# First block of a hybrid decoder: low parts of the weights made by accumulating transfers, head gains applied to the transposed outputs

## The chip, the core and the metric

The kernel runs on one core of a Trainium2 chip. A core has a matmul engine (TensorE, PE in the profile; its weight loads are PEld), a vector engine (VectorE, DVE), a scalar engine (ScalarE, ACT), a general engine (GpSimd, POOL) and a sync engine (SyncE, SP). Each takes its instructions in the order of its own queue. Transfers between DRAM and the core's memory are issued from one of these queues and run beside the engines. The metric is the device time of one execution in microseconds (us); lower is better. The kernel before was run three times.

## What is computed

A decoder trunk of one layer, 2048 tokens, width 1024. The layer has a token mixer (three groups of heads: retention, HGRN2 and GLA, all fed by one input projection and closed by one output projection) and a gated channel mixer with a short convolution. Only the token mixer matters here:

```python
def token_mixer(h, w_in, w_gla_up, b_gla, lb, head_gain, w_out, pos):
    proj = h @ w_in
    (rq, rk, rv, rg, hq, hf, hi, hg, aq, ak, av, ag, alow) = jnp.split(proj, offs, axis=-1)
    ...
    o = jnp.concatenate([o_r, o_h.astype(o_r.dtype), o_a.astype(o_r.dtype)], axis=-1) * head_gain
    return o @ w_out

    # in the layer
    h = rms_norm(x) * (1.0 + sc1) + sh1
    x = x + g1 * token_mixer(h, ...)
```

`head_gain` is a vector over the 1024 columns of `o`, that is, over the rows of `w_out`.

## The kernel before

**Arithmetic.** PE multiplies in a rounded 32-bit format. To keep the precision of 32-bit floats, each operand is split in a high part (the value rounded to that format) and a low part (value minus high part), and each product takes three matmuls: high by high, high by low, low by high (`split3`, lines 244 to 248). So each weight needs a high part, made by ACT as a cast, and a low part, made by DVE as a subtraction.

**Blocks.** The sequence is cut in four blocks of 512 tokens. In each block the mixer's work comes as units, in the order of `ORDER` (line 35): HGRN2 pair 0, GLA, HGRN2 pairs 1 to 3, retention pairs 0 and 1. A unit multiplies its pieces of the input projection by the normalised input `h` (`cf_gemm`, `tf_gemm` and `tf512`), and then runs a chain of smaller matmuls and DVE and ACT steps (`gated` or `retention`) that ends in an output `o`, transposed by PE into `oT` (`transposed`, line 555). The output projection follows in two halves (`out_half`, line 902): the first at the end of the block, the second after the first unit of the next block.

**Pieces.** A piece of weights is 128 x 1024 floats, 512 KB. `piece` (line 212) and, for units that use 512 columns at once, `tf512` (line 286) load it from DRAM into one of two raw buffers (`wraw`), cast it into one of three `whi` tiles and subtract into one of three `wlo` tiles. A `whi` or `wlo` tile comes free when the matmuls of the piece three before are over. The first time that a piece is used, in block 0, its low part is also written to a DRAM scratch by `keep` (line 205, issued on SP); later blocks load the low part from there (`key + "l" in kept`) and no longer subtract. The eight pieces of the output projection are scaled by `head_gain`: ACT makes the high part in four steps of 256 columns with the gain as a scale (L236), DVE the low part in four (L239), both parts are kept, and later blocks load both.

**Other users of the raw buffers.** The adaLN weights (`wada`) pass through the same two raw buffers. `ada` (line 193) has DVE multiply and reduce one of them, and `piece` and `tf512` do one such load and reduction ahead of their own work while the list `later` has entries: eight in block 0 after the first unit, and more in blocks 1 and 2.

**Start.** `startup` (line 376) does the first unit's projections by hand. Eight slices k of `x` are normalised one after another (`scaled`, `high` and `low`: DVE, ACT, DVE), each followed by DVE reductions of adaLN weights (`cond`), and the matmuls of each slice are issued as soon as it and its weights are there. The weights are `f`, `q` (whole), `v0` (slices 0 to 3) and `v1` (slices 4 to 7). `cast` makes a high part, `low_part` a low part. `plan` (line 456) says after which slice each is made: `f` after slice 0, `q` after 1, `v0` after 2, `v1` after 4.

**Order of the instructions.** PE's order is that of the program, everywhere. In the start, that of DVE, ACT and SP is too. Everywhere else a scheduler orders each engine's queue when the program is built, from priorities (`high_priority(offset)` moves the work under it ahead) and from its own idea of durations. POOL has the memsets of attention tiles (`at`, line 606, and `new_qbd`, line 505) in its queue, and issues no transfers.

The a4k tiles hold `oT`, the attention tiles and, in the start, the parts of `v1`; eight of them exist.

Of the kernel before, what the change touches and what calls it, by code (L numbers as in the profile page):

```python
# [9 lines left out]
F32 = mybir.dt.float32  # L10
F32R = mybir.dt.float32r
I32 = mybir.dt.int32
U32 = mybir.dt.uint32
AF = mybir.ActivationFunctionType
ALU = mybir.AluOpType
# [7 lines left out]
NB = SEQ // TB  # L23
# [15 lines left out]
V_BADA, V_BGLA, V_LB, V_HG, V_CW, V_CB, V_FG, NV = 0, 48, 49, 53, 61, 193, 237, 245  # L39
# [15 lines left out]
class Clock:  # L55
# [15 lines left out]
    def adv(self, us):  # L71
        self.t += us
        while self.due and self.due[0][0] <= self.t:
            self._next()
# [26 lines left out]
def trunk(ctx, tc, xT, vecs, cvec, cst, rope, msk, wada, win, walow, wgla, wout, wup, wdown, out):  # L101
    nc = tc.nc
# [15 lines left out]
    def acc_ps(name):  # L118
        return pp.tile([P, 512], F32, tag="acc", name=name, bufs=4)
# [6 lines left out]
    def late_ps(name):  # L126
        return pp.tile([P, 512], F32, tag="late", name=name, bufs=2)
# [10 lines left out]
    V, S, G, T = nc.vector, nc.scalar, nc.gpsimd, nc.tensor  # L138

    vec = pc.tile([P, NV], F32, tag="vec", name="vec")  # L140
# [52 lines left out]
    def ada(m, raw=None):  # L193

        if raw is None:
            raw = ada_load(m, False)
        V.tensor_tensor_reduce(raw[:], raw[:], c_act[:], 1.0, bada1[:, m:m + 1], op0=ALU.mult, op1=ALU.add,
                               accum_out=mod[:, m:m + 1])
# [4 lines left out]
    kept = {}  # L203

    def keep(key, t):

        kept[key] = pdr.tile([P, 1024], F32, tag=f"kept{key}", name=f"kept{key}")
        nc.sync.dma_start(kept[key][:], t.bitcast(F32))

    later = []  # L210

    def piece(src, name, key, gain=None, ahead=50):

        if later:
            ada(later.pop(0))
        with tc.high_priority(offset=ahead):
            hi = pw.tile([P, 1024], F32R, tag="whi", name="h" + name)
            lo = pw.tile([P, 1024], F32R, tag="wlo", name="l" + name)
            if key + "h" in kept:
                nc.sync.dma_start(hi[:].bitcast(F32), kept[key + "h"][:])  # L220
                nc.sync.dma_start(lo[:].bitcast(F32), kept[key + "l"][:])
                return hi, lo
            raw = pw.tile([P, 1024], F32, tag="wraw", name="r" + name, bufs=NRAW)
            nc.sync.dma_start(raw[:], src)
            if gain is None:
                S.copy(hi[:], raw[:])
                if key + "l" in kept:
                    nc.sync.dma_start(lo[:].bitcast(F32), kept[key + "l"][:])
                else:
                    V.tensor_tensor(lo[:], raw[:], hi[:], op=ALU.subtract)  # L230
                    keep(key + "l", lo[:])
            else:
                n = 1024 // len(gain)
                for i, g in enumerate(gain):
                    sl = slice(i * n, (i + 1) * n)
                    S.activation(hi[:, sl], raw[:, sl], AF.Copy, scale=g)  # L236
                for i, g in enumerate(gain):
                    sl = slice(i * n, (i + 1) * n)
                    V.scalar_tensor_tensor(lo[:, sl], raw[:, sl], g, hi[:, sl], op0=ALU.mult, op1=ALU.subtract)  # L239
                keep(key + "h", hi[:])  # L240
                keep(key + "l", lo[:])
        return hi, lo

    def split3(ps, lhs, rhs, first, last, more=False):

        T.matmul(ps, lhs[0], rhs[0], start=first, stop=False, skip_group_check=more)  # L246
        T.matmul(ps, lhs[0], rhs[1], start=False, stop=False, skip_group_check=more)  # L247
        T.matmul(ps, lhs[1], rhs[0], start=False, stop=last, skip_group_check=more)  # L248

    h = [None] * KD  # L250
# [35 lines left out]
    def tf512(name, i):  # L286

        pss = [acc_ps(f"ps{name}_{c}") for c in range(NCH)]
        for q4 in range(4):
            half, sub = q4 // 2, q4 % 2  # L290
            src = win[i + half:i + half + 3:2][:, :, sub * 512:(sub + 1) * 512].rearrange("a p n -> p a n")
            if later:
                ada(later.pop(0))
            with tc.high_priority(offset=50):
                raw = pw.tile([P, 2, 512], F32, tag="wraw", name=f"r{name}_{q4}", bufs=NRAW)
                nc.sync.dma_start(raw[:], src)
                hi = pw.tile([P, 2, 512], F32R, tag="whi", name=f"h{name}_{q4}")
                lo = pw.tile([P, 2, 512], F32R, tag="wlo", name=f"l{name}_{q4}")
                S.copy(hi[:], raw[:])
                key = f"t{i}_{q4}l"  # L300
                flat = lo[:].rearrange("p a n -> p (a n)")
                if key in kept:
                    nc.sync.dma_start(flat.bitcast(F32), kept[key][:])
                else:
                    V.tensor_tensor(lo[:], raw[:], hi[:], op=ALU.subtract)
                    keep(key, flat)
            for c in range(NCH):
                cs = slice(c * P, (c + 1) * P)
                for kk in range(2):
                    k = half * 4 + sub * 2 + kk  # L310
                    sl = slice(kk * 256, (kk + 1) * 256)
                    split3(pss[c][:].rearrange("p (a n) -> p a n", a=2), (h[k][:, 0, cs], h[k][:, 1, cs]),
                           (hi[:, :, sl], lo[:, :, sl]), k == 0, k == KD - 1)
                    adv(3 * M512)
        return pss
# [24 lines left out]
    def sumsq(acc, x, k, name, sl=slice(0, TB), first=None):  # L340
        if k == 0 if first is None else first:
            S.activation(acc[:, sl], x[:, sl], AF.Square)
        else:
            sq = late(f"sq{name}{k}")
            S.activation(sq[:, sl], x[:, sl], AF.Square)
            V.tensor_tensor(acc[:, sl], acc[:, sl], sq[:, sl], op=ALU.add)
# [18 lines left out]
    def x_tile(name, k):  # L365

        if k % 2 == 0:
            pair[0] = px.tile([P, SB], F32, tag="xy", name=name, bufs=4)
        return pair[0][:, (k % 2) * TB:(k % 2 + 1) * TB]
# [6 lines left out]
    def startup():  # L376


        x, W, pending = [], {}, []
# [12 lines left out]
            W[name] = [*t, raw, i]  # L392

        def cast(name):
            S.copy(W[name][0][:], W[name][2][:])

        def low_part(name):
            hi, lo, raw, i = W[name]
            V.tensor_tensor(lo[:], raw[:], hi[:], op=ALU.subtract)

        def cond(m):
            ada(m, raws.pop(m))
# [13 lines left out]
        ps = late_ps("ssn1_0")  # L416
# [7 lines left out]
        ps = late_ps("bcn1_0")  # L424
# [35 lines left out]
        for k, (ld, first, then, wl) in enumerate(plan):  # L460
# [9 lines left out]
            if k in (1, 4):  # L470
                name = "v0" if k == 1 else "v1"
# [83 lines left out]
    def transposed(b, pos, o, name):  # L555

        ps = late_ps("oT" + name)
        for c in range(NCH):
            T.transpose(ps[:, c * P:(c + 1) * P], o[:, c, :], ident)
        oT = pa.tile([P, 2, TB], F32R, tag="a4k", name="oT" + name)  # L560
        S.copy(oT[:, 0, :], ps[:])
        V.tensor_tensor(oT[:, 1, :], ps[:], oT[:, 0, :], op=ALU.subtract)
        oTs[b][pos] = oT

    def attn_out(name, b, attn, v, q, Sst, qn=None):
# [334 lines left out]
        nc.sync.dma_start(d[:, 2:4, :].rearrange("p a n -> p (a n)"), t1[:])  # L900

    def out_half(b, half, acc=None, after_pieces=None):
        hg = [vec[:, V_HG + 4 * half + k:V_HG + 4 * half + k + 1] for k in range(4)]
        ops = [oTs[b][4 * half + k] for k in range(4)]
        for i in range(4):
            wp = piece(wout[half * 4 + i], f"wo{b}_{half}_{i}", f"o{half * 4 + i}", gain=hg, ahead=250 if (b, half) == (0, 0) else 600 if (b, half) == (NB - 1, 1) else 50)
            if i == 3 and after_pieces:
                after_pieces()
            for m in (2 * i, 2 * i + 1):
                if half == 0:  # L910
                    x1[m] = x_tile(f"x1_{b}_{m}", m)
                    nc.sync.dma_start(x1[m], xT[b, :, m, :])
                ps = acc_ps(f"y{b}_{half}_{m}")
                for k in range(4):
                    ws = slice(k * 256 + (m % 2) * P, k * 256 + (m % 2) * P + P)
                    split3(ps[:], (wp[0][:, ws], wp[1][:, ws]), (ops[k][:, 0, :], ops[k][:, 1, :]), k == 0, k == 3)
                    adv(3 * M512)
                with tc.high_priority(offset=HOT):
                    V.scalar_tensor_tensor(x1[m], ps[:], G1[:, m:m + 1], x1[m], op0=ALU.mult, op1=ALU.add)
                if half == 1:  # L920
                    with tc.high_priority(offset=HOT):
                        sumsq(acc, x1[m], m, f"n2_{b}_")
# [116 lines left out]
    for b in range(NB):  # L1039
        pos = 0  # L1040
# [308 lines left out]
    ahead = up_inputs(B)  # L1349
# [109 lines left out]
```

## Time and profile before

| | |
|---|---|
| time, three runs | 2579.37 us median (2577.66 to 2580.24) |
| the profiled execution | 2574.37 us, span of its instructions 2572.6 us |
| PE busy | 2497.9 us, 97% |
| DVE busy | 1986.9 us, 77% |
| ACT busy | 1116.9 us, 43% |
| POOL busy | 144.1 us, 6% |
| memory moved | 533.88 MB, mean 208 GB/s |

A row of a group says: line, engine, operation, output and inputs by the program's names, shapes, count; then the busy time and the mean of one in ns; then how long the engine stood idle ahead of these and what ended the waits. A row of waits says who waited for whom: us in total, times, the longest. A row of a timeline begins with start and duration in us. A row of stages begins with the stretch and its length, and gives busy us and instruction counts of PE, PEld, DVE, ACT and POOL, the granted clock of PE, the mean busy share of the transfer engines and the rate. A row of transfers gives count, size and the median us from issue to landing. The ends of matmuls are modelled.

### The profile page before, as it was taken

What the parts mean: (1) busy time and instruction counts of PE and PEld (TensorE: products, weight loads), DVE (VectorE), ACT (ScalarE), POOL (GpSimd) and SP (SyncE); (2) the same over time, 40 slices, a digit from 0 to 9 for tenths busy, and PEclk for the clock granted to TensorE, in tenths of its full rate; (3) what the DMA queues carried; (4) which work ended last, traced back from release to release, by engine and by line L of the source; (5) the groups of instructions that cost most, each with busy time, mean ns of one, the idle gap of its engine ahead of it and who ended that gap; (6) DMA issues with size and microseconds to landing.
All of it is one profiled execution on the core that took longest, in us unless ns stands there. A gap on an engine that the chain in (4) does not pass through costs nothing.

```text
span 2572.6 us, 37082 instructions
## 1 busy us (share of the span) xinstructions
PE 2497.9 (97%) x13132; PEld 2130.8 (83%) x13132; DVE 1986.9 (77%) x3627; ACT 1116.9 (43%) x1897; POOL 144.1 (6%) x246
## 2 busy tenths in 40 slices
PE   5999999999999999999999999999999999999997
PEld 4798878998889888998778888888878888888886
DVE  8778986868778786887778888887678778778565
ACT  3333434433343234433355554555444554555442
POOL 1000010000000000000010000000000001010000
PEclk9999999999999999999999999999999999999998
DMA  8543656765687856877665445477675544447653
GB/s 304 198 155 132 215 216 231 273 219 178 215 306 269 295 174 213 312 265 258 213 232 175 157 138 167 149 268 247 206 234 166 157 143 148 153 132 266 210 194 115
DMA packets 231753, 533.88 MB, mean 208 GB/s; under 512 B 25072, under 2 KB 26128, under 8 KB 231568
## 3 DMA queue, kind: packets, MB, share of 16 engines
q1 hardware_dynamic: 231568, 531.52, 60.7%
q8 instruction: 103, 1.69, 0.3%
q14 instruction: 82, 0.67, 0.1%
HBM read 397.72 MB, written 133.69 MB: 207 GB/s over the span
## 4 chain that ended last, share of the span: by engine, by line
PE 88%; DVE 7%; DMA 3%; issue 1%; ACT 1%; SPq 0%; DVEq 0%; ACTq 0%
PE X L246 6%; PE X L247 6%; PE X L248 6%; PE lvh L622 4%; PE Z L247 3%; PE Z L246 3%; PE Z L248 3%; PE dX L248 3%; PE dX L246 3%; PE dX L247 3%; PE psqkvgr L248 2%; PE psqkvgr L246 2%; PE psqkvgr L247 2%; PE dY L246 2%; PE dY L248 2%; PE dY L247 2%
## 5 line engine op out<-in xcount | busy, mean ns | idle before, releaser
L246 PE MATMUL X<-B,A 128*128 128x512 f32 x572 | 223.4, 391 | 1.4 <-ACT u L1242 1.4
L247 PE MATMUL X<-B,A 128*128 128x512 f32 x572 | 222.9, 390 | 0.3 <-DMA B<-made 0.3
L248 PE MATMUL X<-B,A 128*128 128x512 f32 x572 | 222.6, 389 | 0.0
L973 DVE TENSOR_TENSOR dA<-rd,dA 128x512 fp32r<-128x512 f32 x154 | 106.1, 689 | 96.3 <-ACT dA L972 96.0
L972 ACT CAST dA<-rd 128x512 fp32r<-128x512 f32 x154 | 95.7, 621 | 154.6 <-PE dY L248 52.6
L973 DVE TENSOR_TENSOR A<-s,A 128x512 fp32r<-128x512 f32 x176 | 120.5, 686 | 40.2 <-ACT A L972 39.9
L246 PE MATMUL psvgh<-hvgh,ha 128*128 128x256 f32 x480 | 139.9, 291 | 0.0
L246 PE MATMUL dX<-dB,dA 128*128 128x512 f32 x352 | 136.9, 389 | 0.0
L247 PE MATMUL dX<-dB,dA 128*128 128x512 f32 x352 | 136.9, 389 | 0.0
L248 PE MATMUL dX<-dB,dA 128*128 128x512 f32 x352 | 136.9, 389 | 0.0
L248 PE MATMUL psvgh<-hvgh,ha 128*128 128x256 f32 x480 | 135.6, 283 | 0.0
L972 ACT CAST A<-s 128x512 fp32r<-128x512 f32 x176 | 108.6, 617 | 62.3 <-PE Z L248 46.8
L247 PE MATMUL psvgh<-lvgh,ha 128*128 128x256 f32 x480 | 135.6, 283 | 0.0
L246 PEld LDWEIGHTS X<-B,A 128*128 128x128 f32 x572 | 107.4, 188 | 24.9 <-ACT u L1242 2.2
L247 PEld LDWEIGHTS X<-B,A 128*128 128x128 f32 x572 | 107.4, 188 | 23.3 <-DMA B<-made 1.4
L248 PEld LDWEIGHTS X<-B,A 128*128 128x128 f32 x572 | 107.4, 188 | 22.4
L246 PE MATMUL Z<-B,A 128*128 128x512 f32 x308 | 120.7, 392 | 2.6 <-ACT B L972 1.7
L622 PEld LDWEIGHTS lvh<-qbh,kh 128*128 128x128 f32 x896 | 115.2, 190 | 7.6 <-issue 1.2
L247 PE MATMUL Z<-B,A 128*128 128x512 f32 x308 | 120.6, 392 | 0.3 <-DVE B L973 0.3
L248 PE MATMUL Z<-B,A 128*128 128x512 f32 x308 | 120.3, 391 | 0.0
L622 PE MATMUL lvh<-qbh,kh 128*128 128x128 f32 x896 | 120.0, 276 | 0.3 <-DVE kh L632 0.3
L973 DVE TENSOR_TENSOR A<-r,A 128x512 fp32r<-128x512 f32 x130 | 89.3, 687 | 30.1 <-ACT A L972 30.1
(440 smaller groups left out, 7102.9 us busy)
## 6 DMA issues: line engine op xcount, KB each, us to landing
gs<-yv SPq DMA_DIRECT2D x154, 256.0 KB, 3.0
rb<-gs SPq DMA_DIRECT2D x154, 256.0 KB, 4.0
r<-wup SPq DMA_DIRECT2D x141, 256.0 KB, 3.3
s<-sumsu SPq DMA_DIRECT2D x132, 256.0 KB, 3.0
wada<-wada SPq DMA_DIRECT2D x48, 512.0 KB, 4.9
rd<-sumsd SPq DMA_DIRECT2D x88, 256.0 KB, 4.0
rd<-wdown SPq DMA_DIRECT2D x66, 256.0 KB, 3.6
x<-xT SPq DMA_DIRECT2D x64, 256.0 KB, 5.2
```

Source lines behind the costliest of these rows:

```text
L246: T.matmul(ps, lhs[0], rhs[0], start=first, stop=False, skip_group_check=more)
L247: T.matmul(ps, lhs[0], rhs[1], start=False, stop=False, skip_group_check=more)
L248: T.matmul(ps, lhs[1], rhs[0], start=False, stop=last, skip_group_check=more)
L622: T.matmul(ps[:, c * P:(c + 1) * P].rearrange("p (h n s) -> p h n s", h=2, s=s), kq[:, c * P:(c + 1) * P], rhs, start=True, stop=True)
L972: S.copy(hi, src)
L973: V.tensor_tensor(lo, src, hi, op=ALU.subtract)
```

## The change

Low parts of weights are made differently where a piece is used for the first time. ACT writes the negative of the high part into the low tile (`S.mul(lo, hi, -1.0)`), and a transfer issued from POOL's queue reads the raw weight from DRAM once more and adds it into that tile (`accum_op=ALU.add`). This applies to `piece`, to `tf512` and, in the start, to `v0` and `v1`; `f` and `q` of the start, and the small `alow`, keep DVE's subtraction.

The weights of the output projection are no longer scaled by the gain. The gain is applied where the outputs of the heads are transposed: the high part of `oT` is a scaled copy out of the accumulator, the low part one DVE instruction that scales and subtracts. The output pieces then go through the same path as the others, and still keep both parts (`both=True`).

```diff
-    def piece(src, name, key, gain=None, ahead=50):
+    def piece(src, name, key, both=False, ahead=50):
...
-            if gain is None:
-                S.copy(hi[:], raw[:])
-                if key + "l" in kept:
-                    nc.sync.dma_start(lo[:].bitcast(F32), kept[key + "l"][:])
-                else:
-                    V.tensor_tensor(lo[:], raw[:], hi[:], op=ALU.subtract)
-                    keep(key + "l", lo[:])
+            S.copy(hi[:], raw[:])
+            if key + "l" in kept:
+                nc.sync.dma_start(lo[:].bitcast(F32), kept[key + "l"][:])
             else:
-                n = 1024 // len(gain)
-                for i, g in enumerate(gain):
-                    sl = slice(i * n, (i + 1) * n)
-                    S.activation(hi[:, sl], raw[:, sl], AF.Copy, scale=g)
-                for i, g in enumerate(gain):
-                    sl = slice(i * n, (i + 1) * n)
-                    V.scalar_tensor_tensor(lo[:, sl], raw[:, sl], g, hi[:, sl], op0=ALU.mult, op1=ALU.subtract)
-                keep(key + "h", hi[:])
+                S.mul(lo[:], hi[:], -1.0)
+                G.dma_start(lo[:], src.bitcast(F32R), accum_op=ALU.add)
+                if both:
+                    keep(key + "h", hi[:])
                 keep(key + "l", lo[:])
...
# tf512
-                    V.tensor_tensor(lo[:], raw[:], hi[:], op=ALU.subtract)
+                    S.mul(lo[:], hi[:], -1.0)
+                    G.dma_start(lo[:], src.bitcast(F32R), accum_op=ALU.add)
...
# startup
         def cast(name):
-            S.copy(W[name][0][:], W[name][2][:])
+            hi, lo, raw, i = W[name]
+            S.copy(hi[:], raw[:])
+            if name in ("v0", "v1"):
+                S.mul(lo[:], hi[:], -1.0)
+                G.dma_start(lo[:], win[i].bitcast(F32R), accum_op=ALU.add)
 
         def low_part(name):
             hi, lo, raw, i = W[name]
-            V.tensor_tensor(lo[:], raw[:], hi[:], op=ALU.subtract)
+            if name in "fq":
+                V.tensor_tensor(lo[:], raw[:], hi[:], op=ALU.subtract)
...
# transposed
-        S.copy(oT[:, 0, :], ps[:])
-        V.tensor_tensor(oT[:, 1, :], ps[:], oT[:, 0, :], op=ALU.subtract)
+        g = vec[:, V_HG + pos:V_HG + pos + 1]
+        S.activation(oT[:, 0, :], ps[:], AF.Copy, scale=g)
+        V.scalar_tensor_tensor(oT[:, 1, :], ps[:], g, oT[:, 0, :], op0=ALU.mult, op1=ALU.subtract)
...
# out_half
-        hg = [vec[:, V_HG + 4 * half + k:V_HG + 4 * half + k + 1] for k in range(4)]
...
-            wp = piece(wout[half * 4 + i], f"wo{b}_{half}_{i}", f"o{half * 4 + i}", gain=hg, ahead=...)
+            wp = piece(wout[half * 4 + i], f"wo{b}_{half}_{i}", f"o{half * 4 + i}", both=True, ahead=...)
```

More of the change, by code (lines that the diff above doesn't have):

```diff
@@ L902, in out_half @@
     def out_half(b, half, acc=None, after_pieces=None):
-        hg = [vec[:, V_HG + 4 * half + k:V_HG + 4 * half + k + 1] for k in range(4)]
         ops = [oTs[b][4 * half + k] for k in range(4)]
         for i in range(4):
-            wp = piece(wout[half * 4 + i], f"wo{b}_{half}_{i}", f"o{half * 4 + i}", gain=hg, ahead=250 if (b, half) == (0, 0) else 600 if (b, half) == (NB - 1, 1) else 50)
+            wp = piece(wout[half * 4 + i], f"wo{b}_{half}_{i}", f"o{half * 4 + i}", both=True, ahead=250 if (b, half) == (0, 0) else 600 if (b, half) == (NB - 1, 1) else 50)
             if i == 3 and after_pieces:
```

## The prediction

> **What bounds the kernel now.** I read the page first: who is busy, and what the chain that ended last consists of.
>
> ```profile
> span 2572.6 us, 37082 instructions
> PE 2497.9 (97%) x13132; PEld 2130.8 (83%) x13132; DVE 1986.9 (77%) x3627; ACT 1116.9 (43%) x1897; POOL 144.1 (6%) x246
> PE 88%; DVE 7%; DMA 3%; issue 1%; ACT 1%; SPq 0%; DVEq 0%; ACTq 0%
> ```
>
> TensorE (PE) sets the time: 88% of the chain is its own. The change takes no matmul away, so it can gain only where PE stands still, and only in the first block, where the low parts are made (later blocks fetch them). Next, busy times by stage. The columns are length, then PE, PEld, DVE, ACT and POOL with their instructions, clock, DMA share, GB/s.
>
> ```profile
> 28.00:58.50 30.50, 25.20 (x139) 21.04 (x139) 26.59 (x41) 7.03 (x10) 2.87 (x3) 1.00 0.89 333
> 58.50:113.00 54.50, 48.60 (x243) 37.88 (x243) 42.00 (x83) 24.42 (x44) 1.99 (x3) 1.00 0.60 209
> 200.00:300.00 100.00, 99.70 (x615) 88.66 (x614) 84.10 (x192) 38.70 (x91) 4.08 (x7) 1.00 0.49 172
> 300.00:400.00 100.00, 93.96 (x557) 80.98 (x556) 85.67 (x213) 36.76 (x67) 8.85 (x14) 0.97 0.60 215
> 290.00:330.00 40.00, 35.79 (x204) 30.87 (x203) 38.88 (x98) 17.68 (x30) 3.01 (x6) 0.96 0.52 182
> ```
>
> The reader is to see two things. From 200 to 300 us PE is 99.7% busy although DVE is at 84%: there relief of DVE buys nothing. From 290 to 330 us DVE is at 97% (38.88 of 40) and PE loses 4.2 us: there it can buy something. Then the waits of PE, in 58.5 to 113 us (first four rows) and in 113 to 400 us (the other six): who was waited for, total, times, longest.
>
> ```profile
> PE psvgg L246 <- ACT hvgg L299: 1.8, 1, 1.8
> PE alg L743 <- ACT snh L707: 1.4, 1, 1.4
> PE psvgg L247 <- DVE lvgg L305: 1.4, 2, 0.8
> PE pshfh L248 <- DVE lhfh L230: 1.3, 1, 1.3
> ...
> PE pshfh L246 <- ACT ha L356: 2.6, 1, 2.6
> PE oTh L559 <- DVE oh L553: 2.4, 1, 2.4
> PE pshfh L247 <- DVE ha L359: 1.6, 1, 1.6
> PE pshfh L248 <- DVE lhfh L230: 1.3, 1, 1.3
> PE bcn L335 <- DVE rsn L158: 1.2, 2, 0.9
> PE oTr L559 <- DVE or L553: 0.8, 1, 0.8
> ```
>
> The lhfh row is one wait at the seam and counts once. So after the start the whole prize is about 14.5 us, 0.6% of the time.
>
> **What is removed.** 34 low parts leave DVE beside the two of the start: 26 of 1024 columns (L230 and L305; two rows shown) and 8 output-weight pieces of four steps each.
>
> ```profile
> L305 DVE TENSOR_TENSOR lqkvgr<-rqkvgr,hqkvgr 128x1024 fp32r<-128x1024 f32 x8 | 9.8, 1220 | 3.6 <-ACT hqkvgr L299 3.6
> L230 DVE TENSOR_TENSOR lvgh<-rvgh,hvgh 128x1024 fp32r<-128x1024 f32 x6 | 7.3, 1217 | 3.2 <-ACT hvgh L226 3.2
> L239 DVE SCALAR_TENSOR_TENSOR lwo<-rwo,vec,hwo 128x256 fp32r<-128x256 f32 x32 | 14.3, 477 | 0.6 <-ACT hwo L236 0.6
> L226 ACT CAST hvgh<-rvgh 128x1024 fp32r<-128x1024 f32 x8 | 8.4, 1052 | 12.1 <-DMA rvgh<-win 10.3 <-issue 1.8
> ```
>
> That is 26 x 1.22 + 14.3 = 46 us of DVE work, spread over 340 us. What it is worth is read from the waits, stage by stage:
>
> - 58.5 to 113 us: three waits come from raw weight, high part and low part in a row: 1.8 + 1.4 + 1.3 = 4.5 us. A raw slot now comes free at the cast and no longer at the subtraction, so the next raw load starts over 1.2 us sooner, and the cast becomes limited by the three-deep ring instead. I take all 4.5 off.
> - Around 130 us: 2.4 us for oh, a DVE product in a dense run that holds low parts of 1.2 us each. I take it off.
> - 313 to 330 us: 2.6 + 1.6 = 4.2 us for the next block's normalised input (ha), in the stretch where DVE is at 97% and which works off lwo as well. Taken off.
> - bcn and oTr, 2.0 us: behind DVE too, but each is a chain of several engines. I take half, 1.0.
>
> Together 12.1 us: the gain, if nothing new waits.
>
> **What is added.** On ACT, one scaled copy of 1024 columns per piece. Its nearest row is the cast at 1052 ns; 36 of them are 38 us, on an engine below 39% in the two long stages, and I cost them at nothing beyond their delay of the low part. Without that cover all 38 us would count. For an output piece four steps on ACT become two, an even trade. On POOL's queue, 36 accumulating transfers of 512 KB. No such transfer is in the trace, so their time from issue to landing, T, is bounded by transfers of the same size:
>
> ```profile
> rvgh<-win SPq DMA_DIRECT2D x8, 512.0 KB, 4.4
> rv<-win SPq DMA_DIRECT2D x2, 512.0 KB, 5.4
> kepti3l<-lv SPq DMA_DIRECT2D x1, 512.0 KB, 6.4
> kepti15l<-lvgh SPq DMA_DIRECT2D x1, 512.0 KB, 2.9
> ```
>
> An accumulation reads DRAM, reads the tile and writes it. If the reads overlap wholly, T is a plain load, 4.4 us; if load and tile read follow one another, 4.4 + 2.9 = 7.3; with a third pass 10.2. I take 7.3, the middle, since two reads are certain. In the crowded start (DMA share 0.89) it is 5.4 + 2.9 = 8.3, at worst 5.4 + 6.4 = 11.8. It costs where a low part is needed soon after its cast. Start, timeline of ACT (first row) and PE:
>
> ```profile
> 41.96 1.03 ACT L395 CAST hv<-rv 128x1024 fp32r<-128x1024 f32 x1
> ...
> 45.45 0.62 PE L446 MATMUL psvgh<-lv,ha 128*128 128x256 f32 x4
> 52.07 0.50 PE L440 MATMUL pshfh<-ha,hf 128*128 128x512 f32 x1 [0.61 <-DVE ha L359]
> 54.82 0.49 PE L440 MATMUL pshfh<-ha,hf 128*128 128x512 f32 x1
> 57.83 0.62 PE L446 MATMUL psvgh<-lv,ha 128*128 128x256 f32 x4
> ```
>
> The second v piece: cast done at 42.99, scaled copy at 44.04, landed at 44.04 + 8.3 = 52.3. PE's order is fixed by hand, and its four matmuls on that low part stood at 45.45; behind them queue the last three k. One k takes 2.75 us (52.07 to 54.82) and some 0.3 for its first matmul, 3.05; so PE ends at 52.3 + 0.52 + 3 x 3.05 = 62.0 instead of 58.45: **+3.5**. DVE is two subtractions shorter there (2.4 us), but is no longer what ends last. At T = 4.4 PE would end at 58.1 (nothing lost), at 11.8 at 65.5 (+7.1).
>
> The next one is ak, the first piece after the start (ACT, then PE):
>
> ```profile
> 58.28 1.04 ACT L226 CAST hakg<-rakg 128x1024 fp32r<-128x1024 f32 x1
> ...
> 64.07 0.40 PE L248 MATMUL psakg<-ha,lakg 128*128 128x512 f32 x1
> ```
>
> Its cast waits for a ring slot of the start and moves with it. Scaled copy done at 60.37, need at 64.07: a lead of 3.7, so PE waits 7.3 - 3.7 = **3.6**. (At 4.4 it is 0.7, at 10.2 it is 6.5.) From then on the ring helps. The cast of a piece starts when the piece three before it has left PE, two pieces ahead of its need:
>
> ```profile
> 150.95 1.05 ACT L226 CAST hvgh<-rvgh 128x1024 fp32r<-128x1024 f32 x1
> ...
> 164.86 0.28 PE L247 MATMUL psvgh<-lvgh,ha 128*128 128x256 f32 x1
> ```
>
> Scaled copy done at 153.05, need at 164.86: 11.8 us of lead. T hides there, with 4.5 us to spare, behind two pieces of matmuls. The keep of a low part on SP now waits for the landing; behind it stand raw loads, which have that same lead. On POOL the memsets of the attention tiles share the queue, but its busy share is 6%.
>
> **Moved.** The 32 transposed outputs take the gain: one operand more in the same two instructions. The nearest DVE form with such an operand is some 60 ns dearer than the present subtraction:
>
> ```profile
> L359 DVE SCALAR_TENSOR_TENSOR ha<-xn,mod,ha 128x512 fp32r<-128x512 f32 x8 | 5.9, 744 | 0.0
> L562 DVE TENSOR_TENSOR oTh<-oTh,oTh 128x512 fp32r<-128x512 f32 x16 | 11.0, 688 | 7.5 <-ACT oTh L561 7.5
> ```
>
> 32 of them are 2 us of DVE spread over four blocks, beside matmuls; uncovered it would be those 2 us.
>
> **The Trainium skill on T.** "DMA: Bandwidth & Descriptors" (Anatomy of one DMA) gives a fixed 2 us plus bytes over 436 GB/s for a transfer issued from GpSimd, 3.2 us for 512 KB, and "Collectives: The Full Stack" (The bandwidth ceiling) says that an add costs because of its two source reads; together an estimate of 4.4 us. The plain loads here already take 4.4, so the trace does not bear out so short a time. By it the sum would be -11, the case "short" below.
>
> **Sum.** +3.5 + 3.6 - 4.5 - 2.4 - 4.2 - 1.0 = -5.0 us. The profiled execution took 2574.4 us, its span and 1.8 around it, and becomes 2569.4. The median of the runs, 2579.4, lies 5.0 above that execution; with the same difference I predict **2574.4**.
>
> **Rivals.** *Short.* T near 4.4: nothing lost at the start, 0.7 at ak, against the 12.1: -11, 2568. For it: two reads on different ports may overlap. Against it: 89% DMA share at the start.
>
> *The ring becomes the bound (slower).* If T exceeds the lead of 11.8, each transfer delays its piece, and as a cast waits for the piece three before, a third of the excess falls on each of some 28 pieces. At T = 12.5: start +7.7, ak +8.8, ring 0.7/3 x 28 = +6.5, and only the 7.6 us after 113 us are gained: +15, 2595. It decides from about T = 10, where start and ak (2T - 8) eat the 12.1. For it: T is unmeasured, and a transfer of this size at the start took 6.4 one way. Against it: 2.9 to 5.4 elsewhere.
>
> *No effect.* DVE's freed time does not reach PE, because what ends last at 130 and 313 us is the transfers or ACT; then 7.1 is lost, 4.5 gained, +2.6: 2582. For it: SP waits long for keeps already, and would hold up the input loads of the next block before 313 us:
>
> ```profile
> SPq L208 <- DVE lvgh L230: 32.7, 4, 12.5
> ```
>
> *Descriptors blocked.* GpSimd must itself prepare these transfers while DVE runs; if each start waits for the DVE instruction in flight, start and ak cost up to 2 x 1.3 = 2.6 more: -2.4, 2577. The longest in flight is of this kind:
>
> ```profile
> 120.83 1.31 DVE L641 COPY_PREDICATED atg<-m_all,lvg 128x512 f32<-128x512 uint32 x1
> ```
>
>  The Trainium skill's "SBUF — State Buffer" (SBUF: two separate sides) describes such a lock for DVE instructions in a two-port mode; no run here shows it.
>
> **How the numbers follow.** Forecast 0.42, short 0.13, ring 0.23, no effect 0.14, blocked 0.08. 0.2% is 5.2 us, about what a measurement of this kernel tells from no change. Faster: short, and somewhat over half of the forecast, whose own spread is -2 to -9, and a little of the rest: 0.42. Same: the rest of the forecast, most of blocked, half of no effect: 0.25. Slower: the ring, and what is left of the others: 0.33. The forecast's own range is 2570 to 2578. The whole range, 2564 to 2595, goes from short with the waits on bcn and oTr gone entirely and some hidden waits besides, to the ring.
>
> **What would show it.** In the changed profile: issue to landing of the accumulations (near 7); PE's wait on lv at 45 us and on lakg, by DMA; no waits on hvgg, lvgg, lhfh, oh and ha; no wait on DMA for low parts after 113 us. It is wrong if low parts are waited for after 113 us, or if DVE gets shorter and the waits on ha stay.

## The result: slower, 2610.9 us

| | kernel before | changed kernel |
|---|---|---|
| median of 4 runs on one chip | 2579.75 us | 2610.89 us |
| lowest and highest | 2577.66, 2580.24 | 2607.49, 2612.71 |
| profiled execution, its span | 2574.37, 2572.6 | 2607.49, 2605.7 |
| busy PE, DVE, ACT, POOL (us) | 2497.9, 1986.9, 1116.9, 144.1 | 2512.3, 1950.5, 1150.3, 180.2 |
| read from DRAM | 397.72 MB | 416.60 MB |

The ratio is 1.0127, 95% interval [1.0112, 1.0142]: 33 us slower (31 by the two medians above), where 5 us faster was forecast and 2595 was the end of the range. Faster by 0.2% is excluded.

### The profile after

First the page of the changed kernel: span, busy engines, and the two transfer queues (packets, MB, share of the 16 transfer engines over the span).

```profile
span 2605.7 us, 37149 instructions
PE 2512.3 (96%) x13132; PEld 2143.6 (82%) x13132; DVE 1950.5 (75%) x3567; ACT 1150.3 (44%) x1909; POOL 180.2 (7%) x282
...
q1 hardware_dynamic: 231568, 531.52, 60.1%
q0 software_dynamic: 6720, 18.88, 4.1%
```

DVE became 36 us shorter (46 were counted). PE executes the same 13132 matmuls, but stands idle for 2605.7 - 2512.3 = 93.4 us in place of 2572.6 - 2497.9 = 74.7, which is 18.7 us more; the other 14.4 of the 33.1 us are longer matmuls (mean granted clock 0.986 in place of 0.993). And there is a new queue, q0. Its 36 accumulations took 4.1% of 2605.7 us on all 16 transfer engines: 2.97 us each.

The same stages as before (length, busy PE, PEld, DVE, ACT, POOL, clock, DMA share, GB/s):

```profile
58.50:113.00 54.50, 44.40 (x205) 34.69 (x204) 28.68 (x59) 23.97 (x32) 6.51 (x6) 0.87 0.83 228
200.00:300.00 100.00, 100.00 (x628) 89.52 (x629) 71.69 (x175) 51.24 (x97) 17.83 (x20) 1.00 0.81 204
300.00:400.00 100.00, 87.94 (x502) 76.86 (x502) 74.86 (x170) 37.44 (x59) 11.12 (x17) 0.94 0.73 226
```

Between 200 and 300 us PE is 100% busy and nothing is lost, as forecast; but look at the last columns. The share of busy transfer engines went from 0.49 to 0.81 while the rate went only from 172 to 204 GB/s: the added transfers hold the engines much longer than their bytes say. From 58.5 to 113 us the share is 0.83 in place of 0.60, and the clock is 0.87 in place of 1.00.

What PE waited for from 58.5 to 113 us (first two rows) and from 113 to 400 us:

```profile
PE psakg L240 <- DMA lakg<-win: 7.4, 1, 7.4
...
PE psvgg L239 <- DMA lvgg<-win: 1.1, 1, 1.1
...
PE y L240 <- DMA lwo<-wout: 4.6, 1, 4.6
PE lvh L621 <- DVE kh L631: 4.5, 1, 4.5
PE uh L660 <- ACT kTh L649: 4.2, 2, 3.4
PE pshfh L239 <- DVE ha L352: 1.8, 1, 1.8
...
PE oTh L557 <- DVE oh L551: 0.3, 1, 0.3
```

The waits that were to go did go: hvgg, the low parts by DVE and lhfh are gone, oh fell from 2.4 to 0.3, ha from 4.2 to 1.8. In their place PE waits for low parts by DMA (lakg 7.4, lwo 4.6, lvgg 1.1), and, what nothing had announced, for DVE's kh and ACT's kTh, which are no part of the change. Where does that come from? In the longest wait on each (4.5 and 3.4 us) DVE or ACT had stood behind a load from DRAM. The group of DVE's reduction of a wada row, from 58.5 to 420 us, in the kernel before (first row) and in the changed one; the last columns are DVE's idle time ahead of it and what ended it:

```profile
L197 DVE CUSTOM_DVE_ANT_0 wada<-wada,c_act,vec 128x1024 f32<-128x1024 f32 x21 | 26.8, 1278 | 8.8 <-DMA wada<-wada 8.8
```

```profile
L197 DVE CUSTOM_DVE_ANT_0 wada<-wada,c_act,vec 128x1024 f32<-128x1024 f32 x19 | 24.3, 1280 | 40.2 <-DMA wada<-wada 24.9 <-issue 15.2
```

DVE, relieved of 36 us of work, stood 31 us longer in front of wada (for 15.2 us of it, "issue", the profile names nothing that was waited for). One such wait, in the timelines of SP's queue (first three rows), DVE and PE of the changed kernel (start, duration):

```profile
299.46 0.32 SPq L208 DMA_DIRECT2D kepto1l<-lwo  x1
299.83 0.43 SPq L208 DMA_DIRECT2D kepto2h<-hwo  x1
300.36 0.89 SPq L190 DMA_DIRECT2D wada<-wada  x1
...
309.24 1.28 DVE L197 CUSTOM_DVE_ANT_0 wada<-wada,c_act,vec 128x1024 f32<-128x1024 f32 x1 [5.01 <-issue]
311.71 0.41 DVE L631 TENSOR_TENSOR kh<-kh,eh 128x256 f32<-128x256 f32 x1
...
312.27 0.98 PE L621 MATMUL lvh<-qbh,kh 128*128 128x128 f32 x3 [4.54 <-DVE kh L631]
```

The load of wada stands in SP's queue behind the store of a low part (kepto1l), which waits until the accumulation of that low part has landed. It is issued at 300.36 and is used at 309.24, 8.9 us later; the two wada loads issued from 285 to 315 us took 8.2 and 8.8 us to land, where the median before was 3.7. The profile names no releaser for DVE's idle 5.0 us here; that it is the load follows from these times. DVE takes its instructions in order, so kh waits behind wada, and PE's matmuls lvh behind kh. Two things can be at work, and the profile alone does not part them: SP's queue is held up, and the load itself takes longer. The largest row of SP's waits from 113 to 420 us shows the first, the median times from issue to landing from 60 to 420 us (kernel before, then changed) the second:

```profile
SPq L208 <- DMA lqkvgr<-win: 53.2, 8, 7.9
```

```profile
wada<-wada SPq DMA_DIRECT2D x21, 512.0 KB, 3.7
rwo<-wout SPq DMA_DIRECT2D x8, 512.0 KB, 4.4
```

```profile
wada<-wada SPq DMA_DIRECT2D x17, 512.0 KB, 5.4
lqkvgr<-win POOLq DMA_DIRECT2D x8, 512.0 KB, 8.2
rwo<-wout SPq DMA_DIRECT2D x8, 512.0 KB, 6.8
lwo<-wout POOLq DMA_DIRECT2D x8, 512.0 KB, 8.0
lvgh<-win POOLq DMA_DIRECT2D x6, 512.0 KB, 5.6
```

Last, what a wait of PE costs beyond its length: stages around the wait on lakg, which ends at 74.12 us.

```profile
66.00:74.00 8.00, 0.72 (x4) 0.24 (x2) 2.59 (x10) 2.68 (x3) 1.52 (x2) 0.73 0.99 250
74.00:78.00 4.00, 3.88 (x9) 3.12 (x10) 0.00 (x0) 0.00 (x0) 0.00 (x0) 0.50 1.06 309
78.00:82.00 4.00, 4.00 (x16) 3.14 (x15) 1.29 (x2) 0.00 (x0) 0.00 (x0) 0.76 0.86 300
82.00:88.00 6.00, 6.00 (x39) 5.37 (x38) 3.97 (x6) 3.24 (x5) 1.21 (x1) 1.00 0.78 242
```

Right after a wait of 7.4 us the granted clock is 0.50, then 0.76, and 1.00 from 82 us on: some 2.0 + 1.0 = 3 us of matmul time are lost after the wait is over. The Trainium skill, "TensorE: Matmul & The Clock Gate" (Part 1), says that the clock falls to half after an idle window of about 3.4 us and comes back after a busy one. The rows agree: half the clock after a wait of 7.4 us, and the full clock from some 6 us later on. A later run has the same drop after a wait of 2.0 us (see the gains, below), which is shorter than that window.

### The profile page after: what moved, and what is told of

The parts are those of the page before. It is cut to its first block, busy times and chain, and to the rows that moved or that the text cites. A ratio compares the mean times of both kernels' runs of the same rounds, so it can differ in the third digit from the quotient of the medians.

```text
span 2605.7 us, 37149 instructions
## 1 busy us (share of the span) xinstructions
PE 2512.3 (96%) x13132; PEld 2143.6 (82%) x13132; DVE 1950.5 (75%) x3567; ACT 1150.3 (44%) x1909; POOL 180.2 (7%) x282
## 3 DMA queue, kind: packets, MB, share of 16 engines
HBM read 416.60 MB, written 133.69 MB: 211 GB/s over the span
## 4 chain that ended last, share of the span: by engine, by line
PE 86%; DVE 6%; DMA 4%; issue 2%; ACT 2%; SPq 0%; POOL 0%; DVEq 0%; POOLq 0%; ACTq 0%
PE X L238 6%; PE X L239 6%; PE X L240 6%; PE lvh L621 3%; PE Z L239 3%; PE Z L238 3%; PE Z L240 3%; PE dX L238 3%; PE dX L240 3%; PE dX L239 3%; PE psqkvgr L240 2%; PE psqkvgr L238 2%; PE psqkvgr L239 2%; PE psvgh L238 2%; PE dY L238 2%
```

## The experiments

Theory A: the stores of low parts on SP's queue wait for the accumulations to land and hold up the loads behind them. Rival B: PE waits for the accumulations as such, whatever SP does. Rival C: the accumulations load the transfer engines, and all other loads land later. The rival that the moved gain costs something was looked at first.

**The gain alone.**

```diff
-                S.mul(lo[:], hi[:], -1.0)
-                G.dma_start(lo[:], src.bitcast(F32R), accum_op=ALU.add)
+                V.tensor_tensor(lo[:], raw[:], hi[:], op=ALU.subtract)
```

(the same in `tf512` and in the start)

> Half of the change alone: the gain moves to the transposed outputs, all low parts stay DVE subtractions. All theories that blame the accumulating transfers expect no loss here: DVE loses 32 x 0.48 and gains 8 x 1.22 us for the output weights, and pays some 2 us on the 32 transposed outputs, so 2574 to 2580, the kernel before (2579.75) at worst. The rival that the moved gain costs something (a dearer step on the path oh, oT, output) expects over 2585.

2579.75 us, ratio 1.0010 [1.0000, 1.0020]. No gain and no loss that can be told from nothing. So the 33 us belong to the accumulations and what goes with them.

**The start without accumulations.** `v0` and `v1` by DVE again, the rest as changed.

> The changed kernel, but v0 and v1 of the start have their low parts from DVE again. Theory A (SP's queue is held up by stores of low parts that wait for the landing): the wait on lv goes (5.1 us at 40 us, 2.5 at the end of the start), and since SP is no longer held 9.1 us for the second v piece, ak's raw load, cast and accumulation come earlier, so part of ak's 7.6 us goes as well; the two stalls at 300 and 376 us stay: 2598 to 2605. Rival B (ak waits for its own accumulation whatever SP does): only the 2.5 us go, 2607 to 2609.

2603.7 us, ratio 1.0104 [1.0081, 1.0127]; its interval overlaps that of the changed kernel. PE's wait on lakg fell from 7.4 to 3.3 us, so part of that wait did come from the start, but the later waits stayed. The start is not the main cause.

**The high part stored in place of the low part.**

```diff
-                keep(key + "l", lo[:])
+                keep(key + "l", hi[:])
```

> The changed kernel, but what is stored under the low parts' names is the high part, so the stores (same bytes, same queue) wait for the cast alone and no longer for the landing; the later blocks therefore multiply by the high part a second time. Theory A: SP's waits at L208 go from 8 us each to 2 or less, the loads behind them come earlier, DVE's idle times ahead of the wada reduction at 309 and 403 us go, with 4.1 + 4.7 + 4.5 us of PE's waits and the clock lost with them, and ak's wait shrinks to 3 to 4 us: 2585 to 2597. Rival B (PE waits for the accumulations as such): SP's waits go, but PE's stay, 2605 to 2611. Rival C (the 18.9 MB more of traffic, or POOL's descriptors): 2605 to 2611 too, with DVE idle before wada as now.

2607.05 us, 1.0114 [1.0094, 1.0133]: no difference that can be told. Taken alone this speaks against theory A. But SP did not become free in this run: the waits for landings were followed by waits for casts, which themselves stood behind late raw pieces (from 60 to 100 us):

```profile
SPq L208 <- ACT hvgg L291: 12.6, 3, 5.7
```

The run moved the wait rather than take it away, so it does not decide.

**The stores off SP's queue.** The edit that does take it away: each low part's store is issued from POOL, behind the accumulation of the next piece.

```diff
+    def release(age=2):
+        turn[0] += 1
+        while held and held[0][0] <= turn[0] - age:
+            keep(*held.pop(0)[1:], q=G)
+    def add_raw(lo, src):
+        with tc.manual_schedule(engines={mybir.EngineType.Pool}):
+            G.dma_start(lo, src.bitcast(F32R), accum_op=ALU.add)
+            release(1)
...
-                keep(key + "l", lo[:])
+                held.append((turn[0], key + "l", lo[:]))
```

> The changed kernel, computing all of it; the stores of accumulated low parts are issued on POOL's queue, each behind the next piece's accumulation, and SP keeps only loads and stores of high parts. Theory A: within 4 us of the run that stores the high part, 2585 to 2600, with no waits of SP's queue on low parts. Rival: the stores now hold up POOL's accumulations instead, the low parts come later still and PE waits for them, 2608 or more.

2595.0 us, 1.0070 [1.0055, 1.0085]. This is 16 us less than the changed kernel (15 by the ratios), with the same traffic. (The edit also takes the order of POOL's transfers from the program.) DVE's idle time ahead of wada fell from 40.2 to 23.0 us, and PE's wait on lakg to 1.8. Theory A holds for about half of the loss. The other half stays although SP waits for no low part any more, and the share of busy transfer engines stays too (0.82 from 200 to 300 us):

```profile
L197 DVE CUSTOM_DVE_ANT_0 wada<-wada,c_act,vec 128x1024 f32<-128x1024 f32 x20 | 25.6, 1281 | 23.0 <-DMA wada<-wada 21.6 <-DMA xn<-xT 1.4
```

**Load that nobody waits for.** The kernel with the gain alone, and for each of the 34 pieces two stores of the high part into places that are never read.

```diff
+    def load(key, t):
+        for c in "ab":
+            d = pdr.tile([P, 1024], F32, tag=f"load{key}{c}", name=f"load{key}{c}")
+            G.dma_start(d[:], t.bitcast(F32))
...
                 keep(key + "l", lo[:])
+                load(key, hi[:])
```

> Load without a wait: the kernel with the gain moved and all low parts from DVE (2579.75), plus two stores of the high part of each of the 34 pieces from POOL's queue into places that nobody reads. Two plain transfers hold the transfer engines about as long as one accumulation did (1.5 us each against 3.0), so the share of busy transfer engines from 200 to 285 us should go from 0.44 to about 0.8 as in the changed kernel, but no engine waits for any of it. Rival C (the traffic as such makes the other loads late): wada's landing goes from 3.4 to about 6 us and the time to 2588 to 2600. Theory A alone (SP held up by waits): 2578 to 2583.

2602.2 us, 1.0092 [1.0074, 1.0109]. No low part is accumulated here, nobody reads what is stored, and some seven tenths of the loss are there all the same. The stage from 200 to 300 us, POOL's queue on the page, and the landings from 60 to 420 us, each in a fence of its own:

```profile
200.00:300.00 100.00, 99.71 (x614) 88.63 (x614) 82.72 (x187) 37.22 (x82) 17.69 (x32) 1.00 0.77 276
```

```profile
q0 software_dynamic: 9792, 35.66, 3.6%
```

```profile
rvgh<-win SPq DMA_DIRECT2D x8, 512.0 KB, 6.1
rwo<-wout SPq DMA_DIRECT2D x8, 512.0 KB, 6.4
```

The 68 plain stores took 3.6% of 2601.7 us: 1.38 us each, so two are 2.8, close to the 2.97 of one accumulation. With the gain alone raw vgh pieces landed in 4.2 us, here in 6.1. Rival C is real, but it works here by another way than wada: DVE stood only 6.5 us in front of wada rows from 58.5 to 420 us (10.7 with the gain alone), while ACT stood 21.1 us in front of four casts of vgg pieces from 58.5 to 113 us, waiting for the raw load (8.9 with the gain alone), and PE's waits on these casts went from 1.8 to 6.2 us.

**Half of that load** (one such store for each piece) **and the same load from ACT's queue** (`nc.scalar.dma_start` in place of `G.dma_start`):

> The run with two unused stores for each piece (2602.2, +22.5 over the gain alone) with one such store instead of two: half the added traffic. If the loss is a matter of traffic by degrees: 2588 to 2594. If it sets in at a threshold (engines near full): under 2585. If it comes from POOL's queue as such and not from the amount: still over 2597.

> The run with two unused stores for each piece (2602.2), these stores issued from ACT's queue instead of POOL's. If the loss of that run is the load on the transfer engines, it stays, 2595 to 2608, with raw pieces landing in about 6 us again (ACT also spends some 0.4 us on each of 68 issues, as SP's issue rows show; 27 us spread over 340 us on an engine below half). If it was POOL's queue or POOL's work on its descriptors: 2580 to 2587.

Half the load: 2584.5 us, 1.0025 [1.0014, 1.0035], with a share of 0.66 from 200 to 300 us; that is 5 us over the gain alone, a fifth of what twice the load cost. The interval overlaps that of the gain alone ([1.0000, 1.0020]), but half of the price of twice the load, 11 us, lies outside it: the price rises faster than the load. The same load from ACT's queue: 2600.0 us, 1.0081 [1.0064, 1.0098]; it is the load on the transfer engines and not POOL's queue or POOL's work. ACT's queue (q10) on the page of that run, and the landing of raw output pieces:

```profile
q10 hardware_dynamic: 9792, 35.66, 3.5%
```

```profile
rwo<-wout SPq DMA_DIRECT2D x8, 512.0 KB, 6.1
```

The Trainium skill, "DMA: Bandwidth & Descriptors" (Queues, rings and completion order), says that each transfer engine takes turns between the queues that have work for it. These runs are in line with it, though they do not show the turns themselves: stores on another queue, which SP never sees, lengthen SP's loads (wada from 4.0 to 5.1 us, rwo from 4.2 to 6.1).

**All waits, an eighth of the added bytes.** The changed kernel with each accumulation cut to 128 columns (in `tf512` and the start too); the other columns of the low part stay the negative of the high part.

```diff
-                G.dma_start(lo[:], src.bitcast(F32R), accum_op=ALU.add)
+                G.dma_start(lo[:, 0:128], src[:, 0:128].bitcast(F32R), accum_op=ALU.add)
```

> The changed kernel, but each accumulation covers only 128 of the 1024 columns (in the other columns the low part stays the negative of the high part). All waits, queues, stores and ACT steps stay; seven eighths of the added load go. If the load is the main cause: 2580 to 2592, with wada and raw pieces landing as before (near 4 us). If the waits for the landings are (time from issue to landing mostly independent of size, SP held as long): 2600 or more. The landing time of these small accumulations tells how much of the 7 to 8 us is the queue's own.

2590.9 us, 1.0041 [1.0026, 1.0055]: 20 us of the loss are gone, 11 stay. POOL's queue on the page, then the landings:

```profile
q0 software_dynamic: 6720, 2.36, 0.9%
...
rvgh<-win SPq DMA_DIRECT2D x8, 512.0 KB, 4.1
lqkvgr<-win POOLq DMA_DIRECT2D x8, 64.0 KB, 3.0
lwo<-wout POOLq DMA_DIRECT2D x8, 64.0 KB, 5.0
lvgh<-win POOLq DMA_DIRECT2D x6, 64.0 KB, 2.7
```

Raw pieces land as before (4.1 us). The accumulations land in 2.7 to 5.0 us, so this run takes away the load and part of the landing time at once; it bounds what the load is worth from above. In engine time it is more than an eighth: 0.9% of 2582.9 us for 36 transfers is 0.65 us each, a fifth of 2.97.

**Both causes taken away.** Accumulations of 128 columns, stores of low parts on POOL's queue.

> Both causes taken away at once: accumulations over 128 of the 1024 columns (the rest of each low part stays the negative of the high part), and the stores of the low parts on POOL's queue behind the next piece's accumulation. If load and SP's held-up queue are the whole loss, what is left is the start and ak with a landing of 3 to 6 us against the gains that were predicted: 2572 to 2582, level with the kernel before or faster. If a third cause is left (ACT's added steps, the clock after waits that stay): 2586 or more, no better than the run with the small accumulations alone (2590.9).

2579.9 us, 1.0005 [0.9996, 1.0014]: level with the kernel before. Load and SP's held-up queue together make up the loss as far as these runs can tell. They do not show that nothing else costs, since DVE's relief stays in this run and can hide a smaller loss (see the gains, below). The two also overlap: 15 to 16 us for SP's queue and 20 to 22 for the load are more than the 31 that there are. One thing stays joined: with the load the landing times of the accumulations fall too, so rival B (PE's own waits on lakg and lwo, 12 us in the changed kernel) is not parted from the load that makes these landings late. The load alone is enough for 20 to 22 us, as the two runs above show.

**Fewer accumulations.** Two runs with the gain moved and the stores of accumulated low parts on POOL: in the first only the four pieces of the first output half are accumulated, in the second all pieces from the second head unit on.

> The gain moved; only the four pieces of the first half of the output projection are made by accumulation (asked for long ahead, used in the stretch where DVE was at 97%), their stores on POOL's queue; all others by DVE. If the relief of DVE at 290 to 330 us is worth what was predicted (4.2 us of waits on ha), and neither SP nor traffic is hurt elsewhere: 2573 to 2577. If traffic makes wada and the next block's loads late there: 2580 to 2585. If the relief does not reach PE: as with the gain alone, 2578 to 2581.

> The run with stores on POOL's queue (2595), but the start, ak, aq and the four vg pieces are DVE subtractions again, as before the change; accumulations begin with the second head unit (first needed near 110 us). If the losses of that run up to 113 us (10.5 us by the offset of the same matmul) belong to the early accumulations alone, the time is 2583 to 2588. If they come back later (what DVE or PE lost there is lost behind anyway): 2592 to 2597.

The four pieces: 2579.7 us, 1.0002 [0.9993, 1.0011]. The waits at 285 to 345 us changed hands, as these rows show (the gain alone, then four accumulations), but the time did not move:

```profile
PE pshqh L237 <- ACT hhqh L225: 7.1, 1, 7.1
```

```profile
PE oTh L577 <- DVE oh L571: 2.0, 1, 2.0
PE oh L594 <- DVE S L688: 2.0, 1, 2.0
PE pshfh L257 <- DVE ha L376: 1.8, 1, 1.8
```

From the second unit on: 2597.8 us, 1.0076 [1.0062, 1.0090], no better than with all pieces accumulated and stores on POOL (2595.0). PE waited 5.1 us for lhfh, an early accumulation of this run. So leaving out those before it did not take the loss away; beyond this wait it was not traced where it came back.

**Without accumulations: a freer SP, fewer stores.** The gain moved, subtractions by DVE; the output weights' high parts no longer stored, or all stores on POOL's queue, or both.

> The gain moved, low parts from DVE, and the high parts of the output weights are no longer stored (they have no gain in them now, so later blocks load the raw piece and cast it on ACT, as they do for the others): 8 stores of 512 KB less in the first block, some 12 us of the transfer engines' time less between 290 and 400 us. If traffic and SP's queue set what is lost there (about 10 us of PE in 300 to 400 us): 2572 to 2577. If what is lost there has other causes: 2578 to 2581; if ACT's added casts in the later blocks cost: over 2582.

> The gain moved, low parts from DVE, and all stores of the first use issued from POOL's queue, so that SP never waits for a low part. Theory A says that a free SP queue lets raw pieces and wada come earlier: the waits on hvgg, lvgg and lhfh and part of those at 325 us go, 2570 to 2576. If the loads are bounded by ring places and traffic and SP's waits for DVE cost nothing: 2578 to 2582.

> The two runs before put together: stores on POOL's queue, and no stores of the output weights' high parts. If both help they add: 2566 to 2573; otherwise as the better of the two.

2580.3 us, 1.0005 [0.9995, 1.0016]; 2585.7 us, 1.0020 [1.0011, 1.0030]; 2580.6 us, 1.0003 [0.9995, 1.0012]. With the load of the kernel before, freeing SP is worth nothing; the run with all stores on POOL's queue alone is 0.2% slower, which no branch of its expectation has. SP's order matters only where the waits in it are long and the loads behind it have no time to spare. No version was faster than the kernel before.

| run | ratio to the kernel before | share of transfer engines, 200 to 300 us |
|---|---|---|
| changed kernel | 1.0127 [1.0112, 1.0142] | 0.81 |
| stores off SP | 1.0070 [1.0055, 1.0085] | 0.82 |
| an eighth of the added bytes | 1.0041 [1.0026, 1.0055] | 0.56 |
| both | 1.0005 [0.9996, 1.0014] | 0.59 |
| load alone, POOL | 1.0092 [1.0074, 1.0109] | 0.77 |
| load alone, ACT | 1.0081 [1.0064, 1.0098] | 0.78 |
| half the load alone | 1.0025 [1.0014, 1.0035] | 0.66 |

## Why the prediction was wrong

**Its landing time was right, its use of it was not.** T was taken as 7.3 us, 8.3 at the start; measured were medians of 5.6 to 8.3 after the start, and 9.4 for the two at the start. That a load and a store one after the other make up this time is not shown: no run looks inside one accumulation, and the agreement may be luck. The case "short" (4.4) did not come about. But the prediction used T only as a delay between a scaled copy and its matmul. The step that failed first is the one that bounded T by "a plain load" plus "a store": it added two times from issue to landing, and never asked how long an accumulation *occupies* the transfer engines. That was 2.97 us each, more than twice a plain transfer's 1.38, and moved the share from 0.49 to 0.81. The row with the old share was quoted in the prediction, and not used. The runs with load alone put this at 20 to 22 us over the gain alone.

**"... behind it stand raw loads, which have that same lead."** This is the second step that failed. Behind the store of a low part on SP's queue stand wada rows too, which DVE needs in order and soon: 8.8 us of idle time became 40.2. Late raw pieces also held up ACT, whose cast then stood ahead of the copy of kTh, and PE waited for that (uh, 3.4 us at this place). ACT in the changed kernel:

```profile
119.23 1.05 ACT L225 CAST hhfh<-rhfh 128x1024 fp32r<-128x1024 f32 x1 [7.91 <-DMA rhfh<-win]
...
124.88 0.58 ACT L649 COPY kTh<-kTh 128x512 f32<-128x512 f32 x1
```

The run with the stores on POOL puts this at 15 to 16 us.

**The start, +3.5.** The mechanism was right and so was the size: the second lv, issued at 43.19, landed after 9.4 us, at 52.6 (forecast 52.3), and the start's last matmuls on lv began at 61.26 in place of 57.83, 3.4 us later. PE also waited 4.3 us for the first lv, until 40.56, which the prediction did not have; that time went from the wait for the second, of which 0.7 us was left. The first matmul behind the start (alg) began 2.5 us later, at 62.36 in place of 59.87, since it waited 0.9 us less for ACT.

**ak, +3.6.** The mechanism was right, the size half of what came. "Its cast waits for a ring slot of the start and moves with it": it moved further. In the changed kernel it stands behind five steps of ACT that wait for the start's sums (SP first, then ACT and POOL, then PE):

```profile
52.71 0.32 SPq L208 DMA_DIRECT2D kepti3l<-lv  x1
...
53.59 0.74 SPq L224 DMA_DIRECT2D rakg<-win  x1
...
61.22 0.60 ACT L705 ACTIVATE sfh<-pshfh 128x512 f32<-128x512 f32 x1 [7.90 <-PE pshfh L438]
...
63.20 1.08 ACT L225 CAST hakg<-rakg 128x1024 fp32r<-128x1024 f32 x1
...
64.40 1.11 ACT L229 ACTIVATE lakg<-hakg 128x1024 fp32r<-128x1024 f32 x1
...
65.81 0.86 POOL L230 DMA_DIRECT2D lakg<-win  x1 [16.88 <-ACT sgh L528]
...
74.12 0.80 PE L240 MATMUL psakg<-ha,lakg 128*128 128x512 f32 x1 [7.40 <-DMA lakg<-win]
```

SP's store of the second lv waited until 52.71, the raw ak piece was asked for at 53.59 in place of 45.86, and its cast came at 63.20 in place of 58.28. The scaled copy was done at 65.51 and needed at 66.72: a lead of 1.2 us in place of 3.7. The transfer took 8.3 us from 65.81, in place of 7.3. So the wait was 7.4, and the slow clock after it added about 3.

**Hidden from 113 us on.** True for 200 to 300 us, where PE is 100% busy. False at 394 us, where PE waited 4.6 us for lwo, a sign of being wrong that the prediction itself had named. The lead of 11.8 us was read from a vgh piece and carried over to the output pieces, whose raw loads were late themselves (ACT stood 6.5 us in front of this one): the scaled copy was done at 385.38 and needed at 390.18, a lead of 4.8.

**The gains, -12.1.** The waits went about as listed (oh to 0.3, ha to 1.8, the others gone), with one exception: bcn was still waited for. The run that takes both causes away shows in its trace what became of them: the same matmul (oTr) starts at 347.66 us in place of 353.57, 5.9 us ahead of the kernel before, but a matmul of alg 39 us further on at 394.41 in place of 392.26, 2.1 us behind. In these 40 us PE waited 3.4 us for DVE, the last 2.0 of them until 384.33, and right after that the granted clock was 0.50 up to about 394.5 us, where the kernel before has 1.00: some 5 us more. So what was gained up to 354 us was lost again, and the time is level. Four accumulations at the place where DVE was at 97% gave nothing either: with the gain alone the waits on ha there had already gone, and one of 7.1 us on a cast stood in their stead; with the four accumulations it gave way to four waits of 6.1 us together (the rows above and 0.3 us on kh). A wait that went was followed by another, and the prediction took each in full.

**A term that was missing.** The prediction counted waits by their length. 14.4 of the 33.1 us are matmuls at a lower clock. Right after the wait on lakg it was 0.50; how much of the rest is due to waits was not measured. The prediction put this term at nothing without a reason.

**The rivals.** "The ring becomes the bound" had the right sign, with the wrong mechanism: its point was T over 10, and T stayed below. "No effect" had the right place ("SP waits long for keeps already, and would hold up the input loads"), priced at 2582 and given 0.14. "Descriptors blocked" stays open: DVE's predicated copy into ath, of the kind quoted there, took 951 ns on average before and 953 after, but whether the transfers' starts waited for such copies was not measured.

## What to carry to other kernels

Price a transfer twice: by the time from its issue to its landing, for what waits for it, and by the time for which it holds the transfer engines, for everything else that is in flight; here the share went from half to four fifths, SP's 512 KB loads landed in 4.7 to 6.8 us in place of 3.7 to 4.6 (medians), and engines that work in order waited for loads that the change never touched. Before a store is made to wait for something slow, list what stands behind it in its queue, with the engine that needs each and when. And taking work off an engine that is busy but rarely waited for bought nothing that lasted, while the engine that takes the work over may be the one that has no room.

## What the hardware showed that was not expected

- An accumulating transfer of 512 KB held the 16 transfer engines for 2.97 us, a plain store of the same size for 1.38, an accumulation of 64 KB for 0.65 (each from its queue's share in the page).
- The price of load was not in proportion: a share of 0.66 from 200 to 300 us went with 5 us over the gain alone, 0.77 to 0.78 with 20 to 22. Whether there is a point at which it sets in stays open.
- An accumulation of 64 KB still took 2.7 to 5.0 us to land, against 5.6 to 8.2 for eight times as much (at a share of 0.56 and 0.81 from 200 to 300 us).
- Stores of low parts that POOL issued landed later than the same ones from SP, also at the low load of the run without accumulations: kepti6l took 5.0 us there, 3.0 in the kernel before. It is not POOL's queue alone: the first four stores of high parts took 2.9 to 3.3 us from POOL in that run, 2.6 to 2.7 from SP before. The cause stays open.
- After a wait of 2.0 us the granted clock was 0.50 for some 10 us (the run with both causes taken away, 384 to 394 us).
